# Two mixing sub-layers of a hybrid encoder: convolution on PE with stacked taps, and another order of the work around it

## The chip, the cores and the metric

One core of one Trainium2 chip runs the whole program in one launch. The time is the device time of one execution in microseconds. TensorE is called PE, VectorE DVE, ScalarE ACT, GpSimd POOL, SyncE SP.

## What is computed

Two encoder layers on 256 tokens of 1024 channels, float32. Each has a mixing sub-layer, and behind it a channel sub-layer: a dense SwiGLU in layer 0, the top 2 of 8 experts in layer 1. The change is in the mixing sub-layers and in what runs beside layer 0's.

```python
mod = silu(c) @ ada_w[l] + ada_b[l]        # six vectors of 1024, "ada" below
shift_m, scale_m, gate_m, shift_f, scale_f, gate_f = split(mod, 6)
h = rms_norm(x, mix_norm_g[l]) * (1 + scale_m) + shift_m
p_pool, p_conv, p_sgu = split(h @ w_in[l])          # 256, 768, 768 wide
# A: windows 2, 4, 8, 16: window mean minus the token, 64x64 map per group, scale
# B: glu = val * sigmoid(gate); y = depthwise conv of 31 taps (+ bias); silu(layer_norm(y))
# C: u, v = split(p_sgu); v = layer_norm(v); u * (sgu_w[head] @ v + sgu_b), chunks of 128 tokens
x = x + gate_m * (concat(A, B, C) @ w_out[l])       # 256 + 384 + 384 wide
```

## The kernel before

All 256 tokens stay on the chip; weights stream in. Channels lie on partitions, tokens run along the row, so a tile of 128 channels is 128 x 256. Products are made in three passes of a rounded type: weights come as 1 MB chunks into a ring of eleven `raw` buffers (`raw_chunk`, L106 to L110), ACT makes the high part (L122), DVE the rest (L123), PE multiplies three times (`mm3`, L131 to L133). Every DMA is issued by SP, in the order in which the program lists it; one that needs a buffer of the ring holds up those behind it.

The order on each engine is recorded by a scheduler that takes the program text as its guide, and in-order from then on: an instruction that waits holds up what stands behind it on its engine. What is written earlier mostly runs earlier; across engines only data and buffers tie things.

`mix_layer` (L327) does the mixing sub-layer of layer `l`. The input projection is done slab by slab: convolution values and gates, the gating branch's v (accumulators `mx`) and u, the pooled branch's slab (`pool_in`, L433). Then:

- **GLU** (L417 to L425): ACT copies the values to `glu` (384 channels as three tiles, each row padded by 15 zeros on either side), ACT makes the sigmoid, POOL multiplies.
- **Gating branch**: `token_norm` of v (L447 to L455; statistics on DVE, addition and power of `rstd_of` on POOL, L137 and L139, then one DVE operation), row sums of the mixing weights (L462), their scaled addition on POOL (L468), the mixing (L501), scale and bias on DVE (L506), the product with u on POOL (L511). `put` (L473 to L475) writes a finished tile as high part (ACT) and rest (POOL).
- **Convolution**: the first `nchain` channel tiles are a chain of 31 multiply-adds on DVE (L517, L522). For the others ACT makes a diagonal 128 x 128 matrix for each tap (L532), and PE accumulates 31 matmuls over shifted rows of `glu` (L536). `nchain` is 1 in layer 0 and 2 in layer 1.
- **Pooled branch**: window sums on POOL (L546 to L564, twelve operations for two tiles), a matmul (L566).
- The convolution's norm turns its tiles to tokens (transposes L576), norms, and back (L582, two groups of three), silu, `put`. Then the output projection in four chunks, row by row into `dn` and `mx`, and the residual.

Beside this run the "ada" products: a vector of 1024 needs eight steps of an accumulation on DVE over 128 x 1024 (`add`, L181 and L184, four 1 MB loads), then a finish: eight narrow matmuls on PE (L204) and small operations. They wait in a queue. `after_chunk` calls `tick(n)` behind each weight chunk, with n from a table (`TICKS0`, `TICKS1`: one entry a chunk); a step counts 1 and a finish 0:

```python
for i in range(KT // 2):
    queue.append((1, lambda i=i: run(i)))
queue.append((0, finish))

def tick(n, done=False):
    while queue and (n or done and not queue[0][0]):
        k, step = queue.pop(0)
        n -= k
        step()
```

Each step is two chunk operations of DVE and one load. In layer 0 the table gives two steps at each of four chunks from the pool slab on; `PRE` and `POST` add steps around the norm behind it.

## Time and profile before

| | |
|---|---|
| median of 3 runs | 1338.85 us (1338.84 to 1339.72) |
| profiled execution | 1339.04 us, span 1336.9 us |
| mean granted clock of PE | 0.984 |
| PE busy | 1277.7 us (96%) |
| DVE busy | 864.4 us (65%) |
| ACT busy | 633.1 us (47%) |
| POOL busy | 78.2 us (6%) |
| DMA | 466.13 MB, mean 349 GB/s |

The span runs from the first to the last instruction; the execution's own time is 2.1 us longer. Busy shares are means over stages: layer 0's mixing lies at about 55 to 136 us, the dense sub-layer at 146 to 340, layer 1's mixing at 340 to 453, the experts behind it.

### The profile page before, as it was taken

To read this page: it belongs to the slowest core of one execution; us is meant where nothing else is said; L and a number is where in the kernel's file an instruction comes from. 1 tells how busy PE (TensorE), PEld (TensorE's weight loads), DVE (VectorE), ACT (ScalarE), POOL (GpSimd) and SP (SyncE) were. 2 spreads that over 40 slices of the span, in tenths; PEclk is the share of its full clock that TensorE was granted. 3 is DMA by queue.
4 is the path that set the end of the run, shared out by engine and by line. 5 is a ranking of instruction groups with operands and counts; after the bars stand their busy time and mean duration, and the time that the engine had idled before them with its cause. 6 is when DMAs were issued, how large, how long until landed. Compare 5 with 4: busy or idle time off the path is not lost.

```text
span 1336.9 us, 17790 instructions
## 1 busy us (share of the span) xinstructions
PE 1277.7 (96%) x6588; PEld 920.6 (69%) x6588; DVE 864.4 (65%) x1036; ACT 633.1 (47%) x897; POOL 78.2 (6%) x106
## 2 busy tenths in 40 slices
PE   6998999999897999999999999999999999999995
PEld 6986899998796878863367873346885336787331
DVE  6799886778799599861069783038886107888102
ACT  3473444344472588851057771036774116676101
POOL 1143100000125100000000000000000000000000
PEclk9998899999998999999999999999999999999998
DMA  9855895986573489899999999999998999999994
GB/s 370 320 206 239 324 400 220 376 300 237 208 284 121 173 300 414 333 375 382 421 421 421 421 377 359 422 421 421 421 421 356 415 421 421 421 420 401 381 422 178
DMA packets 71411, 466.13 MB, mean 349 GB/s; under 512 B 8596, under 2 KB 11284, under 8 KB 18968
## 3 DMA queue, kind: packets, MB, share of 16 engines
q1 hardware_dynamic: 71320, 464.95, 86.7%
q8 instruction: 53, 0.87, 0.3%
q14 instruction: 38, 0.31, 0.1%
HBM read 463.87 MB, written 1.05 MB: 348 GB/s over the span
## 4 chain that ended last, share of the span: by engine, by line
PE 82%; DVE 10%; DMA 3%; ACT 2%; issue 2%; POOL 1%; SPq 0%; DVEq 0%; ACTq 0%; POOLq 0%
PE gu L1080 15%; PE gu L1069 8%; PE dn L933 7%; PE gu L1067 7%; PE gu L1064 7%; PE dn L131 5%; PE dn L132 5%; PE dn L133 5%; PE gu L132 4%; PE gu L133 4%; PE gu L131 4%; DVE cv L522 3%; DVE wl L123 3%; PE mx L1090 2%; PE mx L132 1%
## 5 line engine op out<-in xcount | busy, mean ns | idle before, releaser
L123 DVE TENSOR_TENSOR wl<-raw,wh 128x1024 fp32r<-128x1024 f32 (+1 forms) x454 | 528.0, 1205 | 84.3 <-ACT wh L122 77.0
L122 ACT CAST wh<-raw 128x1024 fp32r<-128x1024 f32 (+1 forms) x454 | 446.0, 1034 | 134.7 <-PE gu L132 42.8
L1080 PE MATMUL gu<-raw,big 128*64 128x512 f32 x896 | 203.0, 594 | 0.0
L1069 PE MATMUL gu<-wl,big 128*128 128x512 f32 x448 | 177.3, 396 | 4.8 <-DVE wl L123 4.8
L1067 PE MATMUL gu<-wh,big 128*128 128x512 f32 x448 | 175.3, 391 | 0.0
L1109 DVE TENSOR_TENSOR maf<-mx,mf 128x256 f32<-128x256 f32 x28 | 11.9, 424 | 225.5 <-PE dn L933 185.2
L1080 PEld LDWEIGHTS gu<-raw,big 128*64 128x64 f32 x896 | 64.1, 137 | 126.1 <-issue 124.7
L1064 PE MATMUL gu<-wh,big 128*128 128x512 f32 x448 | 141.1, 395 | 0.0
L131 PE MATMUL gu<-big,wh 128*128 128x256 f32 x464 | 132.3, 288 | 1.5 <-ACT big L299 1.3
L132 PE MATMUL gu<-big,wh 128*128 128x256 f32 x464 | 131.7, 285 | 0.0
L133 PE MATMUL gu<-big,wl 128*128 128x256 f32 x464 | 131.2, 285 | 0.0
L1083 ACT COPY mg<-gu 128x512 f32<-128x512 f32 x28 | 16.4, 586 | 216.0 <-PE gu L1080 216.0
L933 PE MATMUL dn<-raw,maf 128*64 128x512 f32 x448 | 110.8, 599 | 0.6 <-DVE maf L1109 0.6
L1069 PEld LDWEIGHTS gu<-wl,big 128*128 128x128 f32 x448 | 84.4, 188 | 28.4 <-DVE wl L123 9.8
L184 DVE SCALAR_TENSOR_TENSOR acc<-raw,cond,acc 128x1024 f32<-128x1024 f32 x74 | 97.3, 1314 | 1.0
L1067 PEld LDWEIGHTS gu<-wh,big 128*128 128x128 f32 x448 | 84.4, 188 | 17.2
L1064 PEld LDWEIGHTS gu<-wh,big 128*128 128x128 f32 x448 | 82.8, 189 | 19.5 <-ACT wh L122 2.9
L131 PEld LDWEIGHTS gu<-big,wh 128*128 128x128 f32 x464 | 89.4, 194 | 3.0 <-ACT big L299 2.0
L132 PEld LDWEIGHTS gu<-big,wh 128*128 128x128 f32 x464 | 90.0, 194 | 0.6 <-issue 0.2
L132 PE MATMUL dn<-wl,mah 128*128 128x512 f32 x224 | 89.4, 400 | 0.1
L133 PEld LDWEIGHTS gu<-big,wl 128*128 128x128 f32 x464 | 89.3, 193 | 0.2 <-DVE wl L123 0.2
L133 PE MATMUL dn<-wh,mal 128*128 128x512 f32 x224 | 87.4, 392 | 0.0
(241 smaller groups left out, 1558.7 us busy)
## 6 DMA issues: line engine op xcount, KB each, us to landing
raw<-in_experts SPq DMA_DIRECT2D x336, 1024.0 KB, 13.0
raw<-in_ada_pairs SPq DMA_DIRECT2D x24, 1024.0 KB, 7.3
raw<-in_ada_w SPq DMA_DIRECT2D x16, 1024.0 KB, 9.2
raw<-in_ffn_w_down SPq DMA_DIRECT2D x11, 1024.0 KB, 7.6
raw<-in_ffn_w_gate SPq DMA_DIRECT2D x10, 1024.0 KB, 11.2
raw<-in_ffn_w_up SPq DMA_DIRECT2D x10, 1024.0 KB, 9.2
raw<-in_w_out SPq DMA_DIRECT2D x8, 1024.0 KB, 7.0
raw<-in_in_first SPq DMA_DIRECT2D x8, 768.0 KB, 17.9
```

The costliest lines, as they stand in the source:

```text
L122: behind(lambda: nc.scalar.copy(out=h, in_=s), on_act)
L123: behind(lambda: nc.vector.tensor_tensor(out=l, in0=s, in1=f32(h), op=ALU.subtract), on_dve)
L131: nc.tensor.matmul(out=o, lhsT=lh, rhs=rh, start=first, stop=False, skip_group_check=True)
L132: nc.tensor.matmul(out=o, lhsT=lh, rhs=rl, start=False, stop=False, skip_group_check=True)
L133: return nc.tensor.matmul(out=o, lhsT=ll, rhs=rh, start=False, stop=last, skip_group_check=True)
L184: nc.vector.scalar_tensor_tensor(out=acc[0], in0=c[:, a], scalar=cond[:, k:k + 1], in1=acc[0], op0=ALU.mult, op1=ALU.add)
L522: nc.vector.scalar_tensor_tensor(out=cv[:, ct], in0=glu[:, ct, j:j + S], scalar=cl[:, w0 + j:w0 + j + 1], in1=cv[:, ct], op0=ALU.mult, op1 ...
L933: nc.tensor.matmul(out=ds[0][q * HALF:(q + 1) * HALF], lhsT=a[:, r], rhs=ws[r // 2][:, r % 2, c], start=first, stop=last, skip_group_check ...
L1064: nc.tensor.matmul(out=p, lhsT=eh[:, k], rhs=wh[a2], start=k == 0, stop=False, skip_group_check=True)
L1067: nc.tensor.matmul(out=p, lhsT=el[:, k], rhs=wh[a2], start=False, stop=False, skip_group_check=True)
L1069: nc.tensor.matmul(out=p, lhsT=eh[:, k], rhs=wl[a2], start=False, stop=k == KT - 1, skip_group_check=True)
L1080: nc.tensor.matmul(out=p[h * HALF:(h + 1) * HALF], lhsT=ef[:, k, :HALF], rhs=w[:, a], start=k == 0, stop=k == KT - 1, skip_group_check=True)
```

## The change

1. **Convolution.** `nchain` becomes 0 and 1. The tiles on PE use taps laid out ahead of the launch (`taps`, 1 MB a tile, loaded into `raw`): two taps are stacked on the 128 rows, 64 channels in the columns, so a tile takes 16 matmuls for each half of its channels, the halves in turns. `glu` holds for each half the row twice, the second shifted by one; DVE writes it straight from the accumulators. ACT makes no diagonals. PE's part now stands ahead of the gating branch.
2. **Chunk steps.** `TICKS0` has -8: eight steps at the pool slab, their finishes put off ("owed") until the next tick. "3B" enters the queue with the others; `PRE` and `POST` are gone.
3. **Order and engines.** The pooled sums are written behind the norm of v, `rstd_of`'s addition goes from POOL to DVE, u is read from its accumulator by DVE (no copy), the product with u goes to DVE, three of eight subtractions of `put` too, the gating branch's row sums and mixing use the `mx` banks, and in layer 1 the pool slab moves ahead.

The diff, cut to its core:

```diff
-TICKS0, NCHAIN0 = (0, 0, 0, 0, 0, 0, 0, 0, 2, 2, 2, 2, 0), 1
-TICKS1, NCHAIN1 = (0, 1, 0, 1, 1, 1, 1, 1, 1, 1), 2
+TICKS0, NCHAIN0 = (0, 0, 0, 0, 0, 0, 0, 0, -8, 2, 2, 0, 0), 0
+TICKS1, NCHAIN1 = (0, 1, 0, 1, 1, 1, 1, 1, 1, 1), 1
...
-PRE, POST = 3, 1
...
     def rstd_of(var, more):
         r = small.tile([P, 1], F32, name="rstd")
-        nc.gpsimd.tensor_scalar(out=r, in0=var, scalar1=more, scalar2=EPS,
-                                op0=ALU.add, op1=ALU.add)
+        nc.vector.tensor_scalar(out=r, in0=var, scalar1=more, scalar2=EPS, op0=ALU.add, op1=ALU.add)
         nc.gpsimd.tensor_tensor(out=r, in0=r, in1=mhalf, op=ALU.pow)
...
+    owed = []
+
     def tick(n, done=False):
+        if n < 0:
+            while n and queue:
+                k, step = queue.pop(0)
+                if k:
+                    step()
+                    n += 1
+                else:
+                    owed.append(step)
+            return
+        while owed:
+            owed.pop(0)()
...
-            for ct in range(CT):
-                nc.scalar.copy(out=glu[:, ct, 15:15 + S], in_=ds[ct][0])
...
+            for ct in range(nchain, CT):
+                dgs[ct] = raw_chunk(t["taps"][l, ct], 2 * PAIRT, HALF)
             for ct in range(CT):
                 sg = small.tile([P, S], F32, name="mf")
...
-                nc.gpsimd.tensor_tensor(out=gl, in0=gl, in1=sg, op=ALU.mult)
...
+                for h in range(2):
+                    hs = slice(h * HALF, (h + 1) * HALF)
+                    for o in range(2):
+                        nc.vector.tensor_tensor(out=glu[o * HALF:(o + 1) * HALF, ct, h, 15 - o:15 - o + S],
+                                                in0=vals[ct][0][hs], in1=sg[hs], op=ALU.mult)
...
+            for ct in range(nchain, CT):
+                p = bank()
+                for m in range(PAIRT):
+                    for h in range(2):
+                        nc.tensor.matmul(out=p[h * HALF:(h + 1) * HALF, :S], lhsT=dgs[ct][:, h * PAIRT + m],
+                                         rhs=glu[:, ct, h, 2 * m:2 * m + S], start=m == 0,
+                                         stop=m == PAIRT - 1, skip_group_check=True)
...
             for n in range(NT):
-                token_norm(vn[:, n], ds[n][0])
+                normed = token_norm(vn[:, n], vs[n][0])
+
+            with tc.issue_after(normed.ins):
+                for ct in range(2):
...
+            def put(f, kt):
+                nc.scalar.copy(out=mh[:, kt], in_=f)
+                eng = nc.vector if 2 <= kt < 5 else nc.gpsimd
+                eng.tensor_tensor(out=ml[:, kt], in0=f, in1=f32(mh[:, kt]), op=ALU.subtract)
...
-                nc.gpsimd.tensor_tensor(out=f, in0=f, in1=u[:, ct], op=ALU.mult)
+                nc.vector.tensor_tensor(out=f, in0=us[ct][0], in1=f, op=ALU.mult)
...
-        ada(0, "2", "3A")
+        ada(0, "2", "3A", "3B")
...
-        tick(PRE)
...
-        tick(POST)
```

`tc.issue_after` ties the operations traced inside it to an instruction on that instruction's own engine. `normed` is on DVE and the sums are on POOL, so it gives no tie between them; their place in the text remains.

How the recorded order moves, in three places (line numbers are those of each program; in the changed one L131 to L133 are L130 to L132, L123 is L122, L181 and L184 are L179 and L182).

PE in layer 0, from the end of the pool slab to the first matmuls of the output projection (into `dn`), before:

```order
L462 MATMUL gu<-tok,ones 128x384 x2
L501 MATMUL gu<-tok 128x256 x6
L536 MATMUL gu<-glu,raw 128x256 x62
L566 MATMUL gu<-mf,pw 128x256
L131 MATMUL dn<-wh,big 128x512
```

and in the changed program (L482 is the convolution, L568 the pooled matmul, L543 the row sums, L553 the mixing, L578 the transposes of the convolution's norm):

```order
L482 MATMUL gu<-glu,raw 64x256 x71
L568 MATMUL gu<-pd,pw 128x256
L543 MATMUL mx<-tok,ones 128x384 x2
L553 MATMUL mx<-tok 128x256 x2
L568 MATMUL gu<-pd,pw 128x256
L553 MATMUL mx<-tok 128x256 x2
L578 MATMUL gu<-ident,cv 128x128 x2
L553 MATMUL mx<-tok 128x256 x2
L578 MATMUL gu<-ident,cv 128x128 x4
L130 MATMUL dn<-wh,big 128x512
```

25 more of the convolution's 96 matmuls stand just ahead, among those of the pool slab. The gating branch's row sums and mixing have moved from ahead of the convolution to behind it; 14 matmuls of the projection stand ahead of the second group of transposes back, 82 behind it.

DVE in layer 0, from the statistics of v's second half on, before:

```order
L450 BN_STATS st<-mx 128x6
L522 SCALAR_TENSOR_TENSOR cv<-glu,cols_94,cv 128x256
L123 TENSOR_TENSOR wl<-raw,wh 128x1024
L184 SCALAR_TENSOR_TENSOR acc<-raw,cond,acc 128x1024
L454 TENSOR_SCALAR tok<-mx,mv,rstd 128x384
L184 SCALAR_TENSOR_TENSOR acc<-raw,cond,acc 128x1024
L452 BN_AGGR mv<-st 128x2
L522 SCALAR_TENSOR_TENSOR cv<-glu,cols_94,cv 128x256
L184 SCALAR_TENSOR_TENSOR acc<-raw,cond,acc 128x1024
L454 TENSOR_SCALAR tok<-mx,mv,rstd 128x384
```

and in the changed program, from the GLU on (L444 the GLU, L498 the norm of v, L558 scale and bias of the mixing):

```order
L444 TENSOR_TENSOR glu<-gu,mf 64x256 x12
L494 BN_STATS st<-mx 128x6 x2
L496 BN_AGGR mv<-st 128x2 x2
L136 TENSOR_SCALAR rstd<-mv 128x1 x2
L122 TENSOR_TENSOR wl<-raw,wh 128x1024 x2
L182 SCALAR_TENSOR_TENSOR acc<-raw,cond,acc 128x1024 x8
L179 TENSOR_SCALAR acc<-raw,cond 128x1024
L182 SCALAR_TENSOR_TENSOR acc<-raw,cond,acc 128x1024 x6
L498 TENSOR_SCALAR tok<-mx,mv,rstd 128x384
L182 SCALAR_TENSOR_TENSOR acc<-raw,cond,acc 128x1024
L498 TENSOR_SCALAR tok<-mx,mv,rstd 128x384
L558 SCALAR_TENSOR_TENSOR mf<-mx,cols_94,sgb 64x256 x3
```

The norm of v stood among single chunk steps; now fifteen of them and another stand ahead of it.

POOL in layer 1 from the GLU on, before (L139 after L137 are the powers of v's two halves, L546 and L548 the first pooled sums):

```order
L425 TENSOR_TENSOR glu<-glu,mf 128x256 x3
L137 TENSOR_SCALAR rstd<-mv 128x1
L139 TENSOR_TENSOR rstd<-rstd,mhalf 128x1
L137 TENSOR_SCALAR rstd<-mv 128x1
L139 TENSOR_TENSOR rstd<-rstd,mhalf 128x1
L468 TENSOR_TENSOR sgb<-sgb,res 128x384
L511 TENSOR_TENSOR mf<-mf,tok 128x256
L546 TENSOR_TENSOR tok<-ap 128x271
```

and in the changed program, from the powers of the norm ahead of layer 1 on (L137 is the power of `rstd_of`, L509 to L525 the pooled sums, L549 the addition of the row sums, L538 `put`):

```order
L137 TENSOR_TENSOR rstd<-rstd,mhalf 128x1 x3
L509 TENSOR_TENSOR tok<-ap 128x271
L511 TENSOR_TENSOR tok<-tok 128x269
L523 TENSOR_TENSOR pd<-tok,invc 64x256 x2
L509 TENSOR_TENSOR tok<-ap 128x271
L525 TENSOR_TENSOR pd<-pd,ap 128x256
L511 TENSOR_TENSOR tok<-tok 128x269
L515 TENSOR_TENSOR tok<-tok 128x265
L517 TENSOR_TENSOR tok<-tok 128x256
L523 TENSOR_TENSOR pd<-tok,invc 64x256 x2
L525 TENSOR_TENSOR pd<-pd,ap 128x256
L137 TENSOR_TENSOR rstd<-rstd,mhalf 128x1
```

The first three powers are those of the two halves of the norm ahead of the layer and of the first half of v; the power of v's second half stands behind all twelve pooled sums, and behind it L549 and four L538. Before, both powers of v stood ahead of the first pooled sum.

## Rows read from the trace of the kernel before

**Rows 1.** busy time by stretch, in us (start:end, length, then for each engine its busy us and number of instructions, then the granted clock of TensorE, the share of the DMA engines and GB/s). Of layer 0: what follows its convolution, its output projection, the norm behind it, the dense sub-layer. Of layer 1: what stands ahead of its convolution on PE, and what follows it. Then the experts, to the end.

```profile
102.40:116.00 13.60, 8.89 (x33) 6.51 (x31) 12.32 (x14) 4.41 (x7) 8.31 (x9) 0.75 1.01 419
116.00:136.00 20.00, 20.00 (x88) 15.85 (x86) 18.74 (x18) 7.42 (x13) 4.48 (x3) 1.00 0.18 72
136.00:146.00 10.00, 7.74 (x58) 6.91 (x57) 8.16 (x14) 5.90 (x12) 4.06 (x5) 0.90 0.59 199
146.00:340.00 194.00, 193.85 (x1356) 180.71 (x1355) 153.38 (x153) 80.92 (x96) 0.95 (x1) 0.99 0.80 310
...
376.00:404.50 28.50, 28.50 (x192) 26.71 (x191) 26.93 (x53) 23.21 (x53) 7.43 (x8) 1.00 0.68 258
...
418.00:435.00 17.00, 9.70 (x34) 6.38 (x33) 15.10 (x22) 3.82 (x7) 6.37 (x10) 0.80 0.47 185
...
600.00:1336.90 736.90, 709.88 (x3186) 418.94 (x3186) 375.30 (x395) 317.37 (x404) 2.06 (x4) 0.99 0.97 398
```

**Rows 2.** the timeline of PE in layer 0 (start, us, engine, line, operation, tiles, count; in brackets the idle time before and who ended it). A matmul of plain f32 stands as two instructions.

```profile
71.49 1.45 PE L462 MATMUL gu<-tok,ones 128*128 128x384 f32 x4
...
75.37 26.94 PE L536 MATMUL gu<-glu,raw 128*128 128x256 f32 x124
...
107.36 1.22 PE L566 MATMUL gu<-mf,pw 128*128 128x256 f32 x2 [3.46 <-POOL mf L564]
...
115.64 0.55 PE L582 MATMUL gu<-ident,tok 128*128 128x128 f32 x3
...
135.96 1.84 PE L204 MATMUL gu<-ones_c,acc 128*128 128x1 f32 x16
```

**Rows 3.** the same of layer 1.

```profile
404.51 13.55 PE L536 MATMUL gu<-glu,raw 128*128 128x256 f32 x62
...
423.95 0.79 PE L132 MATMUL dn<-wl,big 128*128 128x512 f32 x1 [5.23 <-DVE wl L123]
...
429.41 0.77 PE L576 MATMUL gu<-ident,cv 128*128 128x128 f32 x5 [2.06 <-DVE cv L522]
...
434.32 0.55 PE L582 MATMUL gu<-ident,tok 128*128 128x128 f32 x3
...
452.90 0.40 PE L133 MATMUL mx<-wh,big 128*128 128x512 f32 x1
```

**Rows 4.** the timeline of PE in the expert stage: matmuls with 64 columns of weights that go in turns to the two halves of the array (16 of them, as 32 instructions).

```profile
586.67 7.09 PE L1080 MATMUL gu<-raw,big 128*64 128x512 f32 x32
```

**Rows 5.** groups of instructions of the whole run, shapes apart (line, engine, operation, tiles, shapes, count, then busy us and mean ns of one, then idle time before).

```profile
L123 DVE TENSOR_TENSOR wl<-raw,wh 128x1024 fp32r<-128x1024 f32 x422 | 497.3, 1222 | 82.4 <-ACT wh L122 75.1 <-PE gu L1069 2.3 <-DMA raw<-in_experts 1.8
...
L184 DVE SCALAR_TENSOR_TENSOR acc<-raw,cond,acc 128x1024 f32<-128x1024 f32 x74 | 97.3, 1314 | 1.0
...
L506 DVE SCALAR_TENSOR_TENSOR mf<-gu,cols,sgb 64x256 f32<-64x256 f32 x12 | 5.8, 481 | 1.5 <-POOL big L475 1.2
...
L450 DVE BATCH_NORM_STATS2 st<-mx 128x6 f32<-128x384 f32 x4 | 2.2, 558 | 0.9 <-PE mx L133 0.9
...
L454 DVE TENSOR_SCALAR tok<-gu,mv,rstd 128x384 f32<-128x384 f32 x4 | 2.7, 677 | 2.3 <-POOL rstd L139 2.3
```

**Rows 6.** the timeline of DVE in layer 0, and from 394 us in layer 1.

```profile
57.76 0.96 DVE L123 TENSOR_TENSOR wl<-raw,wh 128x768 fp32r<-128x768 f32 x1 [1.34 <-ACT wh L122]
...
97.55 5.24 DVE L184 SCALAR_TENSOR_TENSOR acc<-raw,cond,acc 128x1024 f32<-128x1024 f32 x4
...
106.76 5.05 DVE L184 SCALAR_TENSOR_TENSOR acc<-raw,cond,acc 128x1024 f32<-128x1024 f32 x3
...
132.75 1.28 DVE L184 SCALAR_TENSOR_TENSOR acc<-raw,cond,acc 128x1024 f32<-128x1024 f32 x1
...
394.26 11.56 DVE L522 SCALAR_TENSOR_TENSOR cv<-glu,cols,cv 128x256 f32<-128x256 f32 x29
...
410.11 12.65 DVE L522 SCALAR_TENSOR_TENSOR cv<-glu,cols,cv 128x256 f32<-128x256 f32 x16
```

**Rows 7.** the timeline of POOL in layer 0, and from 413 us in layer 1.

```profile
74.18 1.04 POOL L468 TENSOR_TENSOR sgb<-sgb,res 128x384 f32<-128x384 f32 x1 [2.64 <-ACT res L466]
...
102.82 3.35 POOL L562 TENSOR_TENSOR mf<-tok,invc 64x256 f32<-64x256 f32 x2 [13.35 <-PE gu L566]
...
137.86 0.95 POOL L191 MEMSET acc<- 128x1024 f32 x1 [15.98 <-PE gu L204]
138.92 1.12 POOL L137 TENSOR_SCALAR rstd<-ss 128x1 f32<-128x1 f32 x1
...
140.79 0.85 POOL L137 TENSOR_SCALAR rstd<-ss 128x1 f32<-128x1 f32 x1
...
413.78 0.70 POOL L546 TENSOR_TENSOR tok<-ap 128x271 f32<-128x271 f32 x1
...
421.19 0.90 POOL L475 TENSOR_TENSOR big<-mf,big 128x256 fp32r<-128x256 f32 x1
```

**Rows 8.** the timeline of ACT in layer 0, then one row of SP, which issues the DMAs, then the row of the list of DMA issues from 20 to 75 us that goes with it (KB each, us from issue to landing).

```profile
62.16 0.66 ACT L423 ACTIVATE mf<-gu 128x256 f32<-128x256 f32 x2
...
72.33 1.77 ACT L466 ACTIVATE res<-gu,cols 64x128 f32<-64x128 f32 x6
...
31.14 0.33 SPq L109 DMA_DIRECT2D raw<-in_in_pool  x1
...
raw<-in_in_pool SPq DMA_DIRECT2D x1, 1024.0 KB, 15.2
```

More of the change, by code (lines that the diff above doesn't have):

```diff
@@ L362, in pair @@
                 return [(b0[:, 0], 0), (b0[:, 1], 0), (b1[:, 0], 1)]
-            glu = mp.tile([P, CT, S + TAPS - 1], F32, name="glu")
-            nc.gpsimd.memset(glu, 0.0)
+            glu = mp.tile([P, CT, 2, S + TAPS - 1], F32, name="glu")
+            for edge in (slice(0, 15), slice(14 + S, S + TAPS - 1)):
+                nc.gpsimd.memset(glu[:, :, :, edge], 0.0)
+            plain = mp.tile([P, nchain, S + TAPS - 1], F32, name="plain") if nchain else None
+            if nchain:
+                nc.gpsimd.memset(plain, 0.0)
+            dgs, pds = {}, []
             if l:
@@ L374, in mix_layer @@
                 bs = [quads("gu") for _ in range(4)] + [quads("dn")]
-                halves = [(bs[i // 2][:, i % 2], i // 2) for i in range(9)]
-                vals, gates, us = halves[:3], halves[3:6], halves[6:]
+                halves = [(bs[i // 2][:, i % 2], i // 2) for i in range(10)]
+                vals, gates, us = halves[:3], halves[3:6], halves[7:]
                 b0, b1 = bank("mx"), bank("mx")
@@ new lines, in mix_layer @@
+            with tc.issue_after(normed.ins):
+                for ct in range(2):
+                    a = ap[:, ct]
+                    L = S + 15
+                    s2 = sums[:, 0, :S + 16]
+                    nc.gpsimd.tensor_tensor(out=s2[:, :L], in0=a[:, 0:L], in1=a[:, 1:L + 1], op=ALU.add)
+                    s4 = sums[:, 1, :S + 16]
+                    nc.gpsimd.tensor_tensor(out=s4[:, :L - 2], in0=s2[:, 0:L - 2], in1=s2[:, 2:L], op=ALU.add)
+                    if ct == 0:
+                        off = (7, 6)
+                    else:
+                        nc.gpsimd.tensor_tensor(out=s2[:, :L - 6], in0=s4[:, 0:L - 6], in1=s4[:, 4:L - 2],
+                                                op=ALU.add)
+                        nc.gpsimd.tensor_tensor(out=s4[:, :S], in0=s2[:, 0:S], in1=s2[:, 8:S + 8],
+                                                op=ALU.add)
+                        off = (4, 0)
+                    pd = mp.tile([P, S], F32, name="pd", bufs=2)
+                    for h, w in enumerate((s2, s4)):
+                        hs = slice(h * 64, h * 64 + 64)
+                        nc.gpsimd.tensor_tensor(out=pd[hs], in0=w[hs, off[h]:off[h] + S],
+                                                in1=invc[hs, ct], op=ALU.mult)
+                    nc.gpsimd.tensor_tensor(out=pd, in0=pd, in1=a[:, 8:8 + S], op=ALU.subtract)
+                    pds.append(pd)
@@ L525, in mix_layer @@
-            for ct in range(nchain, CT):
-                w0 = C_CW + ct * TAPS
-                dg = []
-                for j in range(TAPS):
-                    if j % 16 == 0:
-                        dt = raw.tile([P, CH], F32, name="raw")
-                    dg.append(dt[:, j % 16 * P:(j % 16 + 1) * P])
-                    nc.scalar.activation(out=dg[j], in_=ident, func=AF.Copy,
-                                         scale=cl[:, w0 + j:w0 + j + 1])
-                p = bank()
-                for j in range(TAPS):
-                    nc.tensor.matmul(out=p[:, :S], lhsT=dg[j], rhs=glu[:, ct, j:j + S],
-                                     start=j == 0, stop=j == TAPS - 1)
-                nc.scalar.activation(out=cv[:, ct], in_=p[:, :S], func=AF.Identity,
-                                     bias=cl[:, C_CB + ct:C_CB + ct + 1])
@@ L567, in mix_layer @@
+            for ct in range(2):
+                p = bank()
+                nc.tensor.matmul(out=p[:, :S], lhsT=pw[:, ct], rhs=pds[ct], start=True, stop=True)
                 f = small.tile([P, S], F32, name="mf")
```

140 lines of the change are left out of this document (53 added, 87 removed).

## The prediction

> **What bounds the kernel now.** I read the busy time by stretch first. It shows four kinds of stretch [rows 1]. While the dense sub-layer runs, PE is busy 193.85 of 194.00 us, so that stretch starts later or earlier as a block. In the experts PE works 709.88 of 736.9 us and the DMA engines are 0.97 busy: that block too moves with its start, unless its weight stream holds it. What can give time are the two stretches behind the convolutions: 102.4 to 116 us, where PE works 8.89 of 13.60 us and DVE 12.32, and 418 to 435 us, where PE works 9.70 of 17.00 and DVE 15.10. There DVE is the bound, and PE waits: 3.46 us for POOL's pooled sums [rows 2], 5.23 us for a weight split of DVE and 2.06 us for DVE's part of the convolution [rows 3]. Ahead of them PE is full: 28.50 of 28.50 us before layer 1's convolution [rows 1].
>
> The second group of transposes (behind the convolution's norm, three matmuls each) marks the end of this work: 115.64 us in layer 0 and 434.32 us in layer 1 [rows 2, 3]. Behind it PE only works off the output projection. I forecast that mark in both layers, then what stands behind it.
>
> **Layer 0, PE.** The 62 full-width matmuls took 26.94 us, 0.4345 each [rows 2]. They become 96 of 64 columns, 48 pairs in turns on the two halves of the array. No such pair of 256 columns stands in the trace. The nearest row has 16 half-width matmuls of 512 columns in 7.09 us [rows 4], 0.886 a pair, 0.443 at half the columns: 48 x 0.443 = 21.3 us. Lower bound: a pair costs what one full-width matmul does, 20.9. Upper: the halves do not overlap, 96 x 0.4345 = 41.7. I take 21.3, because that row is the same form. The gating branch's matmuls go behind it, so it starts where they did, and ends at 71.49 + 21.3 = 92.8 us instead of 102.3 [rows 2].
>
> **Layer 0, DVE.** PE is then not the last; DVE is. Its row in the new order: the GLU as 12 half-partition multiplies straight from the accumulators, two statistics, two weight splits, 15 chunk steps, the first norm of the gating branch, one more step, the second norm. Prices: a 64x256 operation 0.481, a statistic 0.558, a split 1.222, a chunk step 1.31, a norm 0.677 [rows 5, 6]. The GLU starts between 58.7, when the last narrow split ends [rows 6], and 62.16, the first sigmoid of before [rows 8]; ACT's copies ahead of the sigmoids are gone, so 61. Then 61 + 12 x 0.481 = 66.8; statistics and small operations 1.8, 68.6; splits 2.4, 71.0; 16 steps x 1.31 = 21.0, 92.0; two norms 1.4, 93.4. Steps beside POOL's sums took 5.05 / 3 = 1.68 instead of 1.31 [rows 6]; POOL now has its twelve pooled-sum operations here, about six steps' worth: + 2.2, 95.6. That is 2.8 us behind PE's convolution. The row sums now use the banks that these norms free, so they wait for this: half of the 1.45 us of two such matmuls [rows 2], half of ACT's 1.77 [rows 8], POOL's addition of 1.04 [rows 7]: 98.2. Then six mixing operations and three products (taken at 0.481), two statistics with small operations, two splits, two norms: 4.3 + 1.8 + 2.4 + 1.4 = 9.9, the mark at **108.1, 7.5 us earlier**.
>
> Behind the mark now stand 82 product matmuls x 0.227 (88 instructions in 20.00 us [rows 1]) = 18.6, transposes 0.55, two 512-column matmuls of the owed finish (4 x 0.4345 = 1.7) and a row of sums 1.84 [rows 2]: the projection ends at 130.8 instead of 135.96, **-5.2**. The gain shrinks since PE had worked part of this off while DVE was late.
>
> The norm behind it loses POOL's additions of 1.12 and 0.85 us, a memset of 0.95 (it moves ahead) [rows 7] and the chunk step of 1.28 at 132.75 [rows 6]: 4.2 us at most; DVE's two additions come in, and something else is then late. I take **-3.0**, bounds -1.5 and -4.2. One row of sums, 1.84 us [rows 2], leaves the dense sub-layer, where PE is full: **-1.8**. Layer 0: -10.0.
>
> **Layer 1.** The norm ahead of it loses the two POOL additions, 1.97 less DVE's own: **-1.5** (0 to -2). PE's convolution is 32 pairs x 0.443 = 14.2 against 13.55, +0.6 [rows 3, 4]. It now stands ahead of the gating branch's slab. The mixing matmuls stand behind the row sums now: PE reaches the latter at 418.06 + 0.6 - 2.43 (the mixing, from 72.94 to 75.37 [rows 2]) - 1.45 = 414.8. Before that lie 72 matmuls of 256 columns at half of 0.227, 8.2 us, and 1.7 of the owed finish, so the gate's slab ends at 404.9. DVE is not later: it was busy 26.93 us [rows 1], gets eight multiplies (3.8) and loses 31 chain steps of 0.40 [rows 6], half of its chain work.
>
> Here comes what the change puts in the way: on POOL the twelve pooled-sum operations now stand between the power of the first half's norm and that of the second. First power done at about 406; 12 operations of 0.70 to 0.90 [rows 7], 0.82 each, 9.9 us (8.4 if all take 0.70; 12.3 with four at the 1.68 of [rows 7]): 415.9. Second norm 417.1. Behind it in DVE's order wait four splits of the output projection, 4.9, then the same 7.5 us of mixing, statistics and norms as above: 429.5. Four subtractions of POOL (0.90) now stand ahead of the last powers; I take 1.5 of them as not covered: **431.0, 3.3 us earlier**, and as many matmuls follow as before, to 452.90. If the second chain's 31 steps were all on the path it would be more (-5.5); with the longer sums and POOL's subtractions not covered, +1.
>
> **Costed at nothing.** ACT loses its diagonals and copies, but PE never waited on them in the convolution. Five loads of 1 MB come in, at 419 GB/s [rows 1] 2.5 us each. Three go ahead of the pool slab's load, issued at 31.14 and landed 15.2 us later [rows 8]: 46.3 + 7.5 = 53.8, before its use at about 66. If that cover went, each would cost its 2.5. The projection's loads wait for tap buffers; the last would land near 110, with the mark at 108: up to +4, in the range.
>
> **Sum.** -10.0 - 1.5 - 3.3 = -14.8 against the profiled execution of 1339.04 us: 1324.2. The median of the runs is 1338.85, 0.2 less, so **1324**.
>
> **Rivals.** *A, POOL's sums blocked in layer 0.* The pooled operation of 64x256 took 3.35 us for two beside DVE's steps, and the steps 1.68 instead of 1.31: both suffered [rows 6, 7]. If each of the twelve sums waits for a whole chunk step, they take 12 x 1.31 = 15.7 us longer, end near 103, and the addition behind them is at 104 instead of 98: +6, 1330. For: the rows above. Against: neither operation had doubled. The Trainium skill, page "SBUF — State Buffer", section "Who interferes with whom", says that DVE and GpSimd share one port pair under an exclusive lock, and that a DVE operation with two SBUF inputs contends with a GpSimd one that reads SBUF, the loser waiting for the whole instruction; a chunk step has two such inputs, and the trace's 1.68 against 1.31 agrees that they touch, not that one always loses. Chance 0.15.
>
> *B, the weight stream is the bound of the experts.* At 0.97 busy DMA [rows 1] an earlier start gains nothing if the loads cannot start earlier. For: 0.97. Against: the raw buffers are freed by PE and DVE, and the stream's start shifts with them. Then 1337 to 1339. Chance 0.06.
>
> *C, slower: the halves do not overlap at 256 columns.* A pair then costs 2 x 0.4345 = 0.869, 0.426 more than I took. Layer 1 pays all of it 32 times, since PE is full there, layer 0 48 times less the 2.8 us that PE is ahead of DVE: 34.1 - 2.8 = +31.3, so about 1355. The point from which it decides: 80 x - 2.8 = 14.8, x = 0.22, a pair above 0.66 us. For: no row shows the pair at 256 columns, each half loads its own weights. Against: 0.886 at 512 [rows 4]. The Trainium skill, page "TensorEngine Tiling (Array Packing)", section "Tile-to-Partition Mapping", Restrictions, says that column tiling turns off fast weight load, which speaks against this change; the row at 512 columns was taken in that form and shows no such loss, and at half the columns no run here has it. Chance 0.11.
>
> **How the numbers follow.** The forecast has 0.68. Its own range: all lower bounds together (GLU 2 us earlier, norms -4.2 and -2, layer 1's mark -5.5, steps not slowed beside POOL -2.2) make -22.9, 1316, and I give 1315; all upper ones (GLU 1.2 later, loads +4, norms -1.5 and 0, layer 1's mark +1) would make -2.3, and with about half of that 1331. A lies inside its upper end; the range reaches to 1334 for A with late loads, and leaves out B and C, 0.17 together. A difference of 0.2% (2.7 us) is about what a measurement tells from none. Faster: forecast 0.68 + A 0.15 + the better part of B 0.02 = 0.85; same: the rest of B and a little = 0.05; slower: C less the little = 0.10.
>
> **What would show it.** Right: the convolution in 21 us in layer 0 and 14 in layer 1; the marks near 108 and 431; PE's convolution done before DVE's second gating norm; the second norm of layer 1 waiting on POOL from about 407 to 417; dense sub-layer and experts of the same length, less 1.8. Wrong: a pair above 0.66 us; chunk steps or pooled sums that double; PE idle before the projection with DMA as releaser; experts that end where they ended.

## The result and the profile after

The changed kernel took 1330.62 us (median of 4 runs, 1327.69 to 1331.90) against 1339.28 before (4 runs, 1338.84 to 1340.27). The ratio is 0.9923, 95% interval 0.9905 to 0.9941: 8.7 us faster. The profiled execution is the fastest of the four, 1327.69 us with a span of 1325.8, 11.1 less than before; the sums below are made against it. Its beginning was short: the GLU starts at 58.71 us, while in the ten experiments, which begin with the same instructions (one addition on another engine in experiment 6), it starts between 59.0 and 63.3. So kernels are compared below by medians and by lengths between two landmarks, not by times of day. Part of the 11.1 us is this short beginning: the last split ahead of the GLU (128x768) starts at 55.85 us, in the kernel before at 57.76 [rows 6], 1.9 us later.

PE, landmark by landmark (columns as in [rows 2]; in the changed kernel L482 is the convolution, L584 the transposes back, L202 a finish's row of sums, L254 and L301 the beginning of the next part, L131 a product):

```profile
63.86 4.96 PE L482 MATMUL gu<-glu,raw 128*64 128x256 f32 x42
...
69.18 1.08 PE L482 MATMUL gu<-glu,raw 128*64 128x256 f32 x8
...
75.90 15.76 PE L482 MATMUL gu<-glu,raw 128*64 128x256 f32 x142
...
107.43 0.55 PE L584 MATMUL gu<-ident,tok 128*128 128x128 f32 x3 [1.18 <-DVE tok L498]
...
111.85 1.84 PE L202 MATMUL gu<-ones_c,acc 128*128 128x1 f32 x16
...
124.07 0.80 PE L131 MATMUL dn<-wl,big 128*128 128x512 f32 x1 [3.24 <-DVE wl L122]
...
135.64 1.84 PE L202 MATMUL gu<-ones_c,acc 128*128 128x1 f32 x16
...
143.69 0.74 PE L130 MATMUL gu<-big,wh 128*128 128x256 f32 x4 [0.96 <-ACT big L310]
...
147.77 0.28 PE L131 MATMUL gu<-big,wh 128*128 128x256 f32 x1
147.89 0.28 PE L132 MATMUL gu<-big,wl 128*128 128x256 f32 x1
...
334.04 1.84 PE L202 MATMUL gu<-ones_c,acc 128*128 128x1 f32 x16
...
341.41 2.84 PE L254 MATMUL gu<-ones,ident 128*128 128x128 f32 x24
...
346.00 1.50 PE L301 MATMUL gu<-ident,big 128*128 128x128 f32 x12 [0.97 <-ACT wh L121]
...
357.68 1.84 PE L202 MATMUL gu<-ones_c,acc 128*128 128x1 f32 x16
...
374.64 14.04 PE L482 MATMUL gu<-glu,raw 128*64 128x256 f32 x128
...
423.27 0.55 PE L584 MATMUL gu<-ident,tok 128*128 128x128 f32 x3 [0.36 <-DVE tok L498]
...
446.03 1.03 PE L254 MATMUL gu<-x,ident 128*128 128x256 f32 x4
```

The same landmarks of the kernel before that were not shown yet:

```profile
145.63 0.80 PE L131 MATMUL gu<-big,wh 128*128 128x256 f32 x2 [0.37 <-ACT big L299]
...
149.40 0.41 PE L132 MATMUL gu<-big,wh 128*128 128x256 f32 x1
149.61 0.41 PE L133 MATMUL gu<-big,wl 128*128 128x256 f32 x1
...
150.83 1.84 PE L204 MATMUL dn<-ones_c,acc 128*128 128x1 f32 x16
...
347.10 2.84 PE L243 MATMUL gu<-ones,ident 128*128 128x128 f32 x24
...
353.43 1.53 PE L290 MATMUL gu<-ident,big 128*128 128x128 f32 x12 [2.53 <-DVE big L154]
...
456.90 1.03 PE L243 MATMUL gu<-x,ident 128*128 128x256 f32 x4
```

The two marks are the rows at 107.43 and 423.27, 115.64 and 434.32 before [rows 2, 3]. Read downwards, the lead over before is 8.2 us at the first mark, 0.3 at the end of layer 0's projection (135.64 against 135.96), 1.9 at the first product of the dense sub-layer (143.69 against 145.63), 5.7 behind it (341.41 against 347.10), 7.4 at the last transposes ahead of layer 1 (346.00 against 353.43), 11.1 at its mark, 10.9 at the router (446.03 against 456.90). Of the 8.2 us, 1.9 were already there ahead of the GLU, so the mixing won 6.3 up to its mark. **Nearly the whole gain of layer 0's mixing was lost in its projection, where PE waits 3.24 us for a split of DVE.** In the dense sub-layer the lead grows by 3.75 us. One finish less (the row at 150.83 in the kernel before) is 1.7 of it. The other 2.0 are TensorE's clock: the first products there came 0.21 us apart before (granted clock 0.50 from 145.63 to 150.63 us, behind a norm in which PE worked 1.24 us of the 3.00 from 140 to 143), and 0.12 apart in the changed kernel (granted clock 1.00 from 143.69 to 148.69, PE busy 2.71 of the 4.19 us ahead).

Busy time by stretch (columns as in [rows 1]):

```profile
116.00:136.00 20.00, 16.44 (x67) 12.84 (x66) 18.18 (x19) 4.67 (x8) 0.00 (x0) 0.91 1.00 385
...
146.00:340.00 194.00, 194.00 (x1360) 180.62 (x1359) 150.07 (x150) 77.90 (x93) 1.91 (x2) 1.00 0.76 286
...
418.00:435.00 17.00, 16.64 (x72) 13.44 (x72) 10.37 (x22) 9.60 (x16) 3.22 (x5) 0.92 0.57 204
...
600.00:1325.80 725.80, 699.69 (x3137) 416.40 (x3135) 373.69 (x393) 315.98 (x400) 1.09 (x2) 0.99 0.97 399
```

From 116 to 136 us PE is busy 16.44 us, before 20.00, and the granted clock is 0.91, before 1.00. The row from 418 to 435 us does not show the same work as before, since the mark lies 11.1 us earlier; from 407 to 424 us, which does, PE works 12.11 of 17.00 us where it was 9.70. The experts, from the router to the end, take 879.8 us, before 880.0.

DVE, first layer 0, then layer 1 (L444 GLU, L182 and L179 chunk operations, L558 scale and bias of the mixing, L122 a split, L475 the chain, L498 a norm), and the first and last of POOL's twelve pooled sums in either layer:

```profile
55.85 0.95 DVE L122 TENSOR_TENSOR wl<-raw,wh 128x768 fp32r<-128x768 f32 x1
...
58.71 5.24 DVE L444 TENSOR_TENSOR glu<-gu,mf 64x256 f32<-64x256 f32 x12 [1.90 <-ACT mf L437]
...
79.54 9.51 DVE L182 SCALAR_TENSOR_TENSOR acc<-raw,cond,acc 128x1024 f32<-128x1024 f32 x6
...
95.84 1.50 DVE L558 SCALAR_TENSOR_TENSOR mf<-mx,cols,sgb 64x256 f32<-64x256 f32 x3 [4.42 <-POOL sgb L549]
...
114.21 1.05 DVE L179 TENSOR_SCALAR acc<-raw,cond 128x1024 f32<-128x1024 f32 x1
...
117.64 5.24 DVE L182 SCALAR_TENSOR_TENSOR acc<-raw,cond,acc 128x1024 f32<-128x1024 f32 x4
122.80 1.22 DVE L122 TENSOR_TENSOR wl<-raw,wh 128x1024 fp32r<-128x1024 f32 x1
...
380.69 12.97 DVE L475 SCALAR_TENSOR_TENSOR cv<-plain,cols,cv 128x256 f32<-128x256 f32 x25
...
407.86 0.68 DVE L498 TENSOR_SCALAR tok<-mx,mv,rstd 128x384 f32<-128x384 f32 x1 [7.32 <-POOL rstd L137]
```

```profile
76.51 0.87 POOL L509 TENSOR_TENSOR tok<-ap 128x271 f32<-128x271 f32 x1 [8.34 <-ACT ap L453]
...
78.92 2.66 POOL L523 TENSOR_TENSOR pd<-tok,invc 64x256 f32<-64x256 f32 x2
...
92.29 0.72 POOL L525 TENSOR_TENSOR pd<-pd,ap 128x256 f32<-128x256 f32 x1
...
397.06 0.64 POOL L509 TENSOR_TENSOR tok<-ap 128x271 f32<-128x271 f32 x1
...
406.58 0.73 POOL L525 TENSOR_TENSOR pd<-pd,ap 128x256 f32<-128x256 f32 x1
```

The pooled operation of 64x256 in the kernel before, in layer 1, with no chunk operation of DVE beside it:

```profile
411.27 0.69 POOL L562 TENSOR_TENSOR mf<-tok,invc 64x256 f32<-64x256 f32 x1
```

The split that PE waits for (122.80) stands behind six chunk operations from 114.21 on. In layer 1 the second norm waits 7.32 us for POOL, as the order said. In layer 0 the pooled sums last from 76.51 to 93.0, in layer 1 from 397.06 to 407.3.

### The profile page after: what moved, and what is told of

Same layout as the page of the kernel before. It is cut to its first block, busy times and chain, and to the rows that moved or that the text cites. A ratio compares the mean times of both kernels' runs of the same rounds, so it can differ in the third digit from the quotient of the medians.

```text
span 1325.8 us, 17931 instructions
## 1 busy us (share of the span) xinstructions
PE 1269.3 (96%) x6722; PEld 903.3 (68%) x6722; DVE 841.0 (63%) x1025; ACT 603.2 (45%) x794; POOL 55.1 (4%) x73
## 5 line engine op out<-in xcount | busy, mean ns | idle before, releaser
L122 DVE TENSOR_TENSOR wl<-raw,wh 128x1024 fp32r<-128x1024 f32 (+1 forms) x454 | 526.4, 1201 | 87.0 <-ACT wh L121 82.0
L130 PE MATMUL gu<-big,wh 128*128 128x256 f32 x456 | 128.4, 285 | 1.9 <-ACT big L310 1.9
L131 PE MATMUL gu<-big,wh 128*128 128x256 f32 x456 | 129.1, 284 | 0.7 <-DVE big L311 0.7
L132 PE MATMUL gu<-big,wl 128*128 128x256 f32 x456 | 128.6, 283 | 0.0
L182 DVE SCALAR_TENSOR_TENSOR acc<-raw,cond,acc 128x1024 f32<-128x1024 f32 x74 | 96.6, 1306 | 1.1
L131 PE MATMUL dn<-wl,mah 128*128 128x512 f32 x224 | 89.4, 400 | 0.1
L130 PEld LDWEIGHTS gu<-big,wh 128*128 128x128 f32 x456 | 87.1, 193 | 2.8 <-ACT big L310 2.4
L131 PEld LDWEIGHTS gu<-big,wh 128*128 128x128 f32 x456 | 87.5, 192 | 1.7 <-DVE big L311 1.3
L132 PEld LDWEIGHTS gu<-big,wl 128*128 128x128 f32 x456 | 87.6, 192 | 0.0
L132 PE MATMUL dn<-wh,mal 128*128 128x512 f32 x224 | 87.4, 392 | 0.0
```

Source lines behind the costliest of these rows:

```text
L122: behind(lambda: nc.vector.tensor_tensor(out=l, in0=s, in1=f32(h), op=ALU.subtract), on_dve)
L130: nc.tensor.matmul(out=o, lhsT=lh, rhs=rh, start=first, stop=False, skip_group_check=True)
L131: nc.tensor.matmul(out=o, lhsT=lh, rhs=rl, start=False, stop=False, skip_group_check=True)
L132: return nc.tensor.matmul(out=o, lhsT=ll, rhs=rh, start=False, stop=last, skip_group_check=True)
L182: nc.vector.scalar_tensor_tensor(out=acc[0], in0=c[:, a], scalar=cond[:, k:k + 1], in1=acc[0], op0=ALU.mult, op1=ALU.add)
```

## The experiments

Medians stand against 1330.62 of the changed kernel; the kernel before, run beside them, had 1339 to 1340. The 95% interval of a ratio to before is about 2 us to either side, so a difference of 2 to 3 us between two variants is near the noise. As a second measure, the profiled executions from the start of the GLU to the end differ from the changed kernel's by -4.8, +0.3, +27.1, +1.6, +0.2, +2.0, -7.4, +8.9, +2.7 and -0.5 us in the order of the experiments.

**1. The last chunk steps behind the projection's splits.**

```diff
-TICKS0, NCHAIN0 = (0, 0, 0, 0, 0, 0, 0, 0, -8, 2, 2, 0, 0), 0
+TICKS0, NCHAIN0 = (0, 0, 0, 0, 0, 0, 0, 0, -8, 0, 0, 2, 2), 0
```

> The changed kernel with the last four chunk steps of layer 0's mixing (eight chunk operations on DVE) ticked behind the third and fourth chunk of the output projection instead of the first and second, so that DVE's four splits of the projection stand ahead of them. Theory: the output projection of layer 0 ends late (135.6 us, forecast 130.8) because these chunk operations stand ahead of the splits on DVE and themselves wait for the owed finish. Then it ends at about 131 here, PE has no wait of 3.2 us for a split in it, and the whole is 4 to 5 us faster than the changed kernel. Rival: the projection waits for its weights, since the DMA engines were 1.00 busy there, or loses the time to the granted clock (0.91): then its end stays within 1 us of 135.6 and the total within 1 us.

1325.71 us (1321.68 to 1326.75), 4.9 faster. PE's mark and its next landmark behind the projection:

```profile
110.54 0.58 PE L584 MATMUL gu<-ident,tok 128*128 128x128 f32 x3
...
133.19 1.84 PE L202 MATMUL gu<-ones_c,acc 128*128 128x1 f32 x16
```

22.65 us lie between them, with two finishes of 1.3 and 1.7 us inside, where the changed kernel needs 28.21 with the same two (1.7 each). No wait is left, and the granted clock stays 1.00 from 115 us on. The theory holds; the projection's weights, whose last load the changed kernel issues by 86.5 us and which take 14.2 us to land, had long been there.

**2. The old ticks.**

```diff
-TICKS0, NCHAIN0 = (0, 0, 0, 0, 0, 0, 0, 0, -8, 2, 2, 0, 0), 0
+TICKS0, NCHAIN0 = (0, 0, 0, 0, 0, 0, 0, 0, 2, 2, 2, 2, 0), 0
...
-        ada(0, "2", "3A", "3B")
+        ada(0, "2", "3A")
...
-    ada(0, "5")
+    ada(0, "3B", "5")
+        tick(3)
         xn = rms(hold=HOLDF[:2], late=HOLDF[2])
+        tick(1)
```

> The changed kernel with the chunk steps as before the change: two at the pool slab and two behind each of three projection chunks, 3B around the norm; nothing put off. Theory: the eight steps beside the convolution fill DVE while PE convolves and cost the end mark of the convolution's norm (107.4 us) nothing, so that without them the mark stays within 2 us of 107, but the steps then fill the projection and the norm behind it: 3 to 6 us slower than the changed kernel. Rival: the sixteen chunk operations ahead of the norm of v hold up the mark; without them it comes 3 us or more earlier, and the total is equal or less.

1330.23 us (1327.27 to 1333.51): the same. The mark was at 110.98 with the GLU at 60.40, 50.6 us from it (48.7 in the changed kernel), so twelve chunk operations less ahead of the norm of v did not bring it forward: PE's convolution and what hangs on it set it as well. DVE had finished v's second norm at 75.7 us, PE the convolution only at 93.3, and DVE's first operation on the mixing came 36.7 us behind the start of the GLU (37.1 in the changed kernel); what followed, with DVE's splits and chunk operations now among it, took 2.3 us longer than in the changed kernel. The projection then took 17.6 us without a wait, but the norm behind it waited 1.5 and 3.1 us for DVE, and a finish stayed in the dense sub-layer, which took 201.7 us (197.7 in the changed kernel), its first products at a granted clock of 0.50. Neither expectation is right as a whole: the mark part of the theory holds, its loss does not. As written, the new ticks were worth nothing; with the repair of experiment 1 they are worth 4.5.

The same two kernels measure the port between DVE and POOL. POOL's first sum, a pair of half-tile products and the last sum, here with no chunk operation beside them:

```profile
78.19 0.64 POOL L509 TENSOR_TENSOR tok<-ap 128x271 f32<-128x271 f32 x1 [8.34 <-ACT ap L453]
...
79.50 1.34 POOL L523 TENSOR_TENSOR pd<-tok,invc 64x256 f32<-64x256 f32 x2
...
85.91 0.72 POOL L525 TENSOR_TENSOR pd<-pd,ap 128x256 f32<-128x256 f32 x1
```

8.4 us for the twelve sums (78.19 to 86.6) against 16.5 in the changed kernel, where chunk operations ran beside them: a pair took 1.34 here and 2.66 there.

**3. The halves not in turns.**

```diff
-                for m in range(PAIRT):
-                    for h in range(2):
+                for h in range(2):
+                    for m in range(PAIRT):
```

> The changed kernel with the order of the convolution's matmuls turned: all 16 of the first half of a tile's channels, then all 16 of the second, instead of the two halves in turns. Theory: a pair costs 0.454 us (21.8 us for 48 pairs) because neighbours on different halves of the array overlap; in turns no more, 96 matmuls take about 0.43 each, 41 us in layer 0 (+20) and 28 in layer 1 (+14), 30 to 34 us slower than the changed kernel. Rival: the halved columns alone make a matmul cheaper; then the convolution stays at 22 and 14 us and the total within 1 us.

1357.28 us (1356.35 to 1358.40), 26.7 slower. The longest stretch of its convolution in layer 0 (82 matmuls, two instructions each):

```profile
77.94 31.54 PE L482 MATMUL gu<-glu,raw 128*64 128x256 f32 x164
```

0.385 us a matmul; in turns 71 matmuls took 15.76, 0.222. Both layers together 63.4 us of busy PE against 35.8. The overlap is from taking turns, as the theory says; a half-width matmul alone is a little cheaper than the 0.43 that I had put, hence 27 and not 30. Turns change two things at once, the half of the array and the rows of the accumulator; no run parts them.

**4. The pooled sums tied behind POOL's second power.**

```diff
-        nc.gpsimd.tensor_tensor(out=r, in0=r, in1=mhalf, op=ALU.pow)
+        powers.append(nc.gpsimd.tensor_tensor(out=r, in0=r, in1=mhalf, op=ALU.pow))
...
-                return nc.vector.tensor_scalar(out=dst, in0=p, scalar1=mv[:, 0:1], scalar2=r,
-                                               op0=ALU.subtract, op1=ALU.mult)
+                nc.vector.tensor_scalar(out=dst, in0=p, scalar1=mv[:, 0:1], scalar2=r,
+                                        op0=ALU.subtract, op1=ALU.mult)
+                return powers[-1]
```

> The changed kernel with the pooled sums tied behind POOL's power of the second half's norm of v (an operation of POOL) instead of behind the norm itself (an operation of DVE, which orders nothing on POOL). In layer 1 the second norm then runs at about 401 to 402 us instead of 407.9, and the sums from 401 to 411 instead of 397 to 407. Theory (the step as forecast): DVE's four splits and the mixing behind that norm are on the path, so most of the 7.3 us that the norm waited comes back: 4 to 6 us faster than the changed kernel. Rival: the sums themselves become last, because PE's pooled matmuls and the addition of the row sums stand behind them: within 1.5 us of the changed kernel.

1332.75 us (1331.70 to 1334.77), 2.1 slower. PE now waits for the sums, and the mark of layer 1 follows:

```profile
415.53 0.70 PE L571 MATMUL gu<-pd,pw 128*128 128x256 f32 x2 [4.57 <-POOL pd L528]
...
427.70 0.55 PE L587 MATMUL gu<-ident,tok 128*128 128x128 f32 x3 [0.39 <-DVE tok L500]
```

From the last finish of the dense sub-layer to the mark it took 91.3 us, 89.2 in the changed kernel. The rival's mechanism was right, at 0.6 us more than it allowed: whichever comes second on POOL is waited for.

**5. The pooled sums ahead of v.** The block of the twelve operations moves ahead of v's slab, without a tie.

```diff
+            for ct in range(2):
+                a = ap[:, ct]
...
             if l:
                 slab(t["in_last"][3], CW, 4, vs, tokens=True)
...
-            with tc.issue_after(normed.ins):
-                for ct in range(2):
-                    a = ap[:, ct]
...
```

> The changed kernel with the pooled sums written ahead of the gating branch's v (ahead of its slab in layer 1), so that POOL does them at 376 to 390 us in layer 1, where it was idle, and the power of v's second half no longer stands behind them; the orders of PE and DVE are the same as in the changed kernel. Theory: the 7.3 us that the second norm of v waits for POOL are partly on the path (the tied variant only put the sums themselves on it): that norm comes at 401 to 404, the mark of layer 1 (second group of transposes back) 2.5 to 4 us earlier than in the changed kernel from the same start, and the whole 2.5 to 4 us faster. Rival: PE's slabs and the row sums, which PE reaches at 406.7 only, set the mark anyway, or DVE's chain steps slow down beside POOL by as much as is gained: within 1 us.

1329.98 us (1329.02 to 1330.77), 0.6 faster by the medians; the mark of layer 1 came 87.4 us behind the last finish of the dense sub-layer instead of 89.2. DVE in layer 1 (chain steps, then the second norm of v):

```profile
381.33 0.86 DVE L475 SCALAR_TENSOR_TENSOR cv<-plain,cols,cv 128x256 f32<-128x256 f32 x1
...
385.61 14.99 DVE L475 SCALAR_TENSOR_TENSOR cv<-plain,cols,cv 128x256 f32<-128x256 f32 x25
...
408.09 0.68 DVE L521 TENSOR_SCALAR tok<-mx,mv,rstd 128x384 f32<-128x384 f32 x1 [0.66 <-POOL rstd L137]
```

The norm's wait fell from 7.32 to 0.66 us, but single chain steps beside POOL took 0.86 instead of 0.47, the run of 25 took 14.99 instead of 12.97, three splits took 1.39 to 1.49 instead of 0.95, and so the norm came only 2.1 us earlier. Between the two expectations: the wait was on the path, and the slower operations of DVE beside POOL's took most of it back. The 1.8 us at the mark are clearer than the 0.6 of the medians.

**6. rstd_of's addition back on POOL.**

```diff
-        nc.vector.tensor_scalar(out=r, in0=var, scalar1=more, scalar2=EPS, op0=ALU.add, op1=ALU.add)
+        nc.gpsimd.tensor_scalar(out=r, in0=var, scalar1=more, scalar2=EPS, op0=ALU.add, op1=ALU.add)
```

> The changed kernel with the addition of rstd_of back on POOL. Theory: the addition is on the chain of each norm; POOL took 0.55 us for it where DVE takes 0.14 to 0.22 and is waited for once less, so the norm between layer 0's mixing and its dense sub-layer and the one ahead of layer 1 get 0.8 to 1.6 us longer each, and the marks of both mixings some tenths: 2 to 4 us slower than the changed kernel. Rival: the norms' gain (1.6 and 1.7 us) came from the chunk steps and the memset that went away there: within 1 us.

1333.30 us (1331.07 to 1334.08), 2.7 slower, as the theory said in sum. Not all of its places, though: the norm behind layer 0's mixing was no longer (4.5 us from the last finish to the first transposes in both), the one ahead of layer 1 was 1.5 us longer and layer 1's mixing up to its mark 0.8. In layer 0 the mark came 1.2 us earlier from the GLU's start and the projection took 2.6 longer; the cause of that stays open. So what was won in the former is not the addition's; the chunk step and the memset, which also went away there, are left as its source, not tried by themselves.

**7. Both repairs (1 and 5).**

> The changed kernel with both repairs: the last four chunk steps at the third and fourth projection chunk (as in the late variant, measured 4.9 us faster than the changed kernel) and the pooled sums ahead of v (sums-first variant). Theory: the two act in different layers and add up: 4.5 us plus what the sums-first variant gains, 7 to 9 us faster than the changed kernel, about 1322. Rival: only the first one counts: 4 to 5 us.

1323.55 us (1321.11 to 1323.88), ratio to before 0.9862 (0.9838 to 0.9886): 7.1 faster than the changed kernel, 16.5 faster than before. The two add up (4.9 and, by the medians, 0.6; by the mark of layer 1, 1.8), and this version beats both kernels.

**8. One tile of layer 0 back on DVE's chain.**

```diff
-TICKS0, NCHAIN0 = (0, 0, 0, 0, 0, 0, 0, 0, -8, 2, 2, 0, 0), 0
+TICKS0, NCHAIN0 = (0, 0, 0, 0, 0, 0, 0, 0, -8, 2, 2, 0, 0), 1
```

> The changed kernel with one channel tile of layer 0's convolution back on DVE as a chain of 31 multiply-adds (as before the change), the other two on PE with stacked taps. Theory: DVE is as much the bound as PE up to the mark of layer 0, so the chain's 31 steps of 0.45 to 0.66 us (14 to 20 us) come on top less DVE's idle 10 us there, although PE convolves 7 us less: the mark 6 to 12 us later, the whole 5 to 12 us slower than the changed kernel. Rival: PE's convolution was the bound; with a third of it gone the chain hides in DVE's idle time: within 2 us or faster.

1339.65 us (1337.26 to 1342.05), 9.0 slower: the whole gain is gone (ratio to before 0.999, 0.9976 to 1.0004). The mark came 7.6 us later from the GLU's start (119.57 from 63.29), though PE had convolved a third less. PE now waits 16.07 us for DVE's norm of v ahead of the row sums. DVE is as much the bound as PE; with one tile left on it nothing of the gain remains.

**9. The owed finish early.**

```diff
+            tick(0)
             sb = small.tile([P, 512], F32, name="res", bufs=2)[:, :CW].rearrange("p (c q) -> p c q", c=CT)
```

> The changed kernel with the owed finishes run once ahead of the row sums, behind the pooled sums (the ticks as in the change), so that on DVE the last eight chunk operations no longer stand behind the operations on the finish; in DVE's recorded order they now stand right behind the second norm back, still ahead of three splits of the projection. Theory: not the chunk operations' number but their late start (114.2 us, 6.8 behind the mark, for the finish on PE at 110 to 113.7) made PE wait in the projection. Then they start right behind the second norm, PE has no wait of 3.2 us, and the projection takes 3 to 5 us less behind the mark, which itself comes up to 1.7 later (the finish's two matmuls now stand ahead of the row sums): 1.5 to 4 us faster than the changed kernel. Rival: their place ahead of the splits is enough: the projection takes as long as in the changed kernel (28.2 us from the mark), and the whole is equal or up to 2 us slower.

1333.49 us (1331.42 to 1334.39), 2.9 slower. PE from the mark on:

```profile
112.04 0.55 PE L585 MATMUL gu<-ident,tok 128*128 128x128 f32 x3
...
119.31 0.80 PE L131 MATMUL dn<-wl,big 128*128 128x512 f32 x1 [1.69 <-DVE wl L122]
119.91 0.63 PE L132 MATMUL dn<-wh,big 128*128 128x512 f32 x1
120.34 0.63 PE L130 MATMUL dn<-wh,big 128*128 128x512 f32 x1
```

The chunk operations started right behind the second norm (111.90), and the wait fell to 1.69 us; but behind it the matmuls came 0.43 us apart instead of 0.23 until 124.6, the granted clock from 120 to 125 us being 0.51, and the projection's last product began 27.7 us behind the mark, 28.0 in the changed kernel, with 4.0 and 3.4 us of finishes and other matmuls among the products. The mark itself came 1.6 us later from the GLU's start. So the rival was right on the projection: the earlier start halved the wait, and the clock took back what that gave; that the place ahead of the splits is what costs agrees with experiment 1. Most of the 2.9 us, however, came behind the projection: the dense sub-layer took 200.1 us instead of 197.7, with a wait of 1.13 us for DVE instead of 0.48 and its first products 0.21 us apart at a granted clock of 0.50 (147 to 152 us). Neither expectation had that.

**10. No chain in layer 1, with both repairs.**

```diff
-TICKS1, NCHAIN1 = (0, 1, 0, 1, 1, 1, 1, 1, 1, 1), 1
+TICKS1, NCHAIN1 = (0, 1, 0, 1, 1, 1, 1, 1, 1, 1), 0
```

> The kernel with both repairs, and in layer 1 all three channel tiles of the convolution on PE (no chain on DVE). Theory: ahead of layer 1's row sums PE is full (28.50 of 28.50 us), so the 16 more pairs, 7.1 us, come on top, less what the end of the chain gives DVE: 3 to 7 us slower than the kernel with both repairs. Rival: the chain, 31 dependent steps of 0.47 to 0.86 us beside POOL's sums (19 us), is the bound there: equal or up to 3 us faster.

1328.43 us (1327.40 to 1329.72), 4.9 slower than with one chain: PE is full ahead of layer 1's row sums (50.50 us busy of the 50.50 from 359 us on), so what leaves DVE there lands on the path. From the last transposes ahead of layer 1 to the row sums it took 67.6 us, with one chain 61.0; the convolution alone took 20.94 and 14.04.

## Why the prediction was right, and where not

Forecast 1324 us in 1315 to 1334; measured 1330.6. The mechanism and most terms were right. One term, what stands behind layer 0's mark, was mis-sized by 5 us; without it the forecast would have been about 1329. That the other terms then fit so well is in part luck: TensorE's clock, which stood in no term, gave 2.0 us, and the short beginning of the profiled execution 1.9.

- **The convolution: right.** 48 pairs at 0.443, 21.3 us, and 14.2 in layer 1; measured 4.96 + 1.08 + 15.76 = 21.8 and 14.04. The row of 512 columns [rows 4] carried over to 256. Rival C, which experiment 3 makes real, costs 27 us: its sign and its size were about right, its condition is not met.
- **The mark of layer 0: the number in part by luck.** Forecast 108.1, measured 107.43, with GLU 5.24 us for 5.8, chunk operations beside POOL 9.51 / 6 = 1.59 for 1.68. But the GLU started at 58.71, not 61; from its start to the mark it took 48.7 us, 47.1 was forecast, and in experiments 4 and 5 it took 48.6 and 49.0. "PE is then not the last; DVE is" was not so: PE's convolution (to 91.7), DVE's norms (to 91.4) and POOL's sums (to 93.0) end together. DVE's first operation on the mixing came 4.4 us behind its second norm, 2.6 was forecast, and from there to the mark it took 11.6 us for 9.9, with a wait of 1.84 for a power on POOL. Experiment 2 shows that taking from DVE alone gains nothing, experiment 8 that adding to it costs; relieving POOL or PE alone was not tried in this layer.
- **What stands behind the mark: wrong.** The step was "Behind it PE only works off the output projection", priced by 82 products at 0.227. I had counted the eight chunk operations nowhere in it, though the recorded order has them on DVE ahead of the projection's splits. PE waited 0.32 + 3.24 us, and seven matmuls behind the wait ran at nearly twice their time. -5.2 was forecast at the projection's end, -0.3 came. Experiment 1 gives 4.9 of it back by moving these operations behind the splits (a finish moves with them), experiment 9 shows that an earlier start alone does not, and the forecast's length from the mark to the last row of sums (130.8 - 108.1 = 22.7 us) is what experiment 1 has (22.65).
- **The norm behind it:** -3.0 forecast, -1.6 measured; by experiment 6 the addition has no part in it.
- **The dense sub-layer:** -1.8 forecast, -3.75 measured. One finish left it, as forecast (six ran there before, five now), worth 1.7; the other 2.0 are the higher granted clock of its first products, which the forecast did not have.
- **The norm ahead of layer 1:** -1.5 forecast, -1.7 measured, 1.5 of it the addition (experiment 6).
- **Layer 1: right.** -3.3 forecast, -3.6 measured, with two finishes in it before and after; the sums took 10.2 us for 9.9 and the norm waited 7.32. That the wait was on the path was right, but experiments 4 and 5 show that only part of it can be taken away: experiment 5 brings the mark 1.8 us forward, to about -5.5, the size of the forecast's better bound.
- **Rival A:** its mechanism is real, its place was not. The argument against it, "neither operation had doubled", was a misreading: with no chunk operation beside it the same operation took 0.69 us in that trace (411.27), with one 1.68 [rows 7]. In the changed kernel the sums doubled, which the prediction had named as a sign of being wrong. POOL lost 8.1 us to the chunk operations (16.5 against 8.4), half of the 15.7 that I gave, but the sums ended 1.4 us behind the convolution, and the addition behind them waited for ACT 1.8 us longer anyway. The Trainium skill, page "SBUF — State Buffer", section "Who interferes with whom", says that a DVE instruction with two SBUF inputs contends with a GpSimd instruction that reads SBUF, under an exclusive lock; the doubled pair (2.66 for 1.34) agrees in kind. A single sum took 0.9 us longer, less than a whole chunk operation (1.31).
- **Rival B:** not so; the experts took 879.8 us from the router on, 880.0 before.

## What to carry to other kernels

When work is moved ahead of a bottleneck, what is left of it stands somewhere too: look in the recorded order at what now stands ahead of each operand of the next full stretch, and count it there. Where three engines end together, a step that relieves one of them can be worth nothing until the others follow (experiment 2), and an operation moved to an idle engine is not free if it slows the engine that is the bound (experiment 5). When a landmark is forecast, compare it from the start of its own stretch: a short beginning can make a wrong length look right.
